# Down projection: sums of activations by way of HBM, and 25 groups by seven products in place of 22

## The chip, the cores and the metric

The kernel runs on one core of one Trainium2 chip. The metric is the device time of one execution in microseconds (us). Five engines work in parallel, each through its own instructions in order: PE (TensorE, the matrix products), DVE (VectorE), ACT (ScalarE), POOL (GpSimd) and SP (SyncE); the last two here mostly issue DMA transfers. [...]

## The reference, cut to what matters

One block of a transformer, float32, 256 tokens, width 2048. The change touches its last part, the gated feed-forward with a causal convolution over three tokens:

```
h2 = rms_norm(x, g_ffn[l])
u = causal_depthwise_conv(h2 @ w_up[l], conv_w[l], conv_b[l])   # w_up: 2048 x 11264
u_gate, u_val = jnp.split(u, 2, axis=-1)
x = x + (jax.nn.silu(u_gate) * u_val) @ w_down[l]               # w_down: 5632 x 2048
```

Ahead of it stand three attentions, their gates and an output projection; they stay as they are.

## The kernel before, in words

**Precision.** Each float32 operand is split into a high part (cast to fp32r on ACT, "hi") and a low part (the rest, a subtraction on DVE, "lo"). A product is three matmuls: activation high x weight high, activation low x weight high, activation high x weight low. In the down projection the function `three` writes them (L1309, L1310, L1311), and `parts` writes the cast (L1304) and the subtraction (L1305) for each piece of weights, up to 128 x 1024 elements.

**Up projection** (L1207 on). 176 pieces of `w_up`, 512 KB each, are loaded by SP, split, and multiplied (L1219, L1221). After each 8 pieces the generator `conv` does the convolution of two blocks of 256 channels: `u` is the input, `y` the result, `g` the gate times the value. The high and the low part of `g` go to `aT`, the activations, which stay on the chip.

**Down projection** (PLANS, from L1245 on). The 5632 rows of `w_down` are 22 pairs of 256 rows; the 2048 output columns are two halves of 1024 (`nb` 0 and 1). So there are 44 groups (a pair, a half), each with two weight tiles of 128 x 1024. A group is done in one of two ways:

- by eight (`eight`): two tiles of rows, two halves of tokens, two halves of columns, 8 products, 24 matmuls, two loads of 512 KB, in two steps of 12 matmuls.
- by seven (`seven`): 7 products of sums in place of 8, 21 matmuls, in four steps `u0` to `u3` of 3, 6, 6 and 6 matmuls. It needs four sums of weights (T1 and T3 in one tile of 128 x 1024, T4 and T2 in another) and four sums of activations (`forms`: FS1 to FS4). Its four pieces are p0 (512 columns), p1 (1024), and the two tiles of sums.

The strings in PLANS give the order of groups, "e" by eight and "s" by seven: 8 and 14 by seven, 22 by eight.

**Sums of weights.** `weight_sums` (L1170) loads the two tiles of a group during the up projection, adds them on DVE (L1181) and writes the results to HBM through POOL (`T`). A new one begins every 7 pieces of `w_up`. All 22 groups by seven get T4 and T2 so. Twelve of them (ALL_FOUR) get T1 and T3 as well; for the other ten DVE makes T1 and T3 in the down projection by two additions (L1371, L1372), into a buffer `t13`.

**Sums of activations.** `forms(p)` makes them in the down projection: five DVE operations on the split activations (L1273 to L1277), two casts on ACT, two subtractions on DVE (L1284, L1285). The results lie in `sf` and in parts of `aT` that are not needed any more.

**What sets the order.** `steps` is a list of (prep, use). The preparation of a step (load, cast, subtraction) is written two steps ahead of its use (AHEAD = 2), and `keep` fixes loads, casts and DVE operations in the order in which they are written. Beyond that an engine runs as far ahead as its buffers let it. There are four buffers for high parts and four for low parts (SBUFS = 4, tags "hi" and "lo"): the cast of one piece waits until PE has used the piece that stands four places before it. Raw weights have four buffers (WBUFS = 4), and from the eleventh load on some more (tag "more"). The matmuls are not held to the written order; a scheduler places them when the program is built.

Of the kernel before, what the change touches and what calls it, by code (L numbers as in the profile page):

```python
# [37 lines left out]
PLANS = ("eeeee" + "se" * 5 + "sse" + "s" + "eee", "e" + "sse" * 4 + "ssse" + "sssee")  # L38
ALL_FOUR = {(0, 6), (0, 7)} | {(1, p) for p in range(14) if p not in (4, 6, 8, 11)}
# [10 lines left out]
NSEVEN = tuple(plan.count("s") for plan in PLANS)  # L50


@with_exitstack
def hybrid_block(
# [1075 lines left out]
    def conv(ps, f, s):  # L1130
# [23 lines left out]
        else:  # L1154
# [9 lines left out]
            ended.append(f)  # L1164

    ended = []
    made = {}
    asked = [(0, p) for p in range(NSEVEN[0])] + [(1, p) for p in range(NSEVEN[1])]

    def weight_sums(nb, p):  # L1170
# [11 lines left out]
        four = (nb, p) in ALL_FOUR  # L1182
        add(r[0][:, 0], r[0][:, 1])
        if four:
            add(r[0][:, 1], r[1][:, 1])
# [3 lines left out]
        made[nb, p] = [dram.tile([P, PIECE], F32, name=f"T{j}_{nb}_{p}") for j in range(1 + four)]  # L1189
        if four:  # L1190
            nc.gpsimd.dma_start(made[nb, p][1], r[0].rearrange("p b n -> p (b n)"))
# [15 lines left out]
    for f0 in range(0, FT, 4):  # L1207
        for s in range(2):
            pairs = [two_banks(f"u{f0 + i}_{s}") for i in (0, 2)]
            c0 = s * D_FF + f0 * P  # L1210
            for k in range(0, KT, 2):
# [11 lines left out]
                if asked and n_ticks[0] > 8 and n_ticks[0] % 7 == 2:  # L1223
                    adding.append([weight_sums(*asked.pop(0)), 0])
# [22 lines left out]
    FS3, FS1, FS2, FS4 = range(4)  # L1247
# [8 lines left out]
    def form_of(p, f):  # L1256
        if f == FS4:
            return pieces_of(p)[:, 0, :, 1]
        if p < 10:
            return sf[:, p, f]  # L1260
        return pieces_at(31 - p).rearrange("p k (f l q) -> p (k f) l q", f=2, l=2)[:, f]

    def forms(p):

        flat = aT[:, 2 * p : 2 * p + 3].rearrange("p k s -> p (k s)").bitcast(F32)
        v = flat[:, :1024].rearrange("p (k l t q) -> p k l t q", k=2, l=2, t=NT)
        d = sm.tile([P, 512], F32, tag="junk", bufs=2, name=f"fd_{p}").rearrange("p (f l q) -> p f l q", f=2, l=2)
        r = down_pool().tile([P, 512], F32, tag="fr", bufs=1, name=f"fr_{p}").rearrange("p (f q) -> p f q", f=4)
        g = rbc.rearrange("p (k q) -> p k q", k=2)
        two = flat[:, : 2 * 640].rearrange("p (a b) -> p a b", b=640)[:, :, :512]  # L1270
        two = two.rearrange("p a (l t q) -> p a l t q", l=2, t=NT)[:, :, :, 0]
        tt = nc.vector.tensor_tensor
        keep(tt(d, two, v[:, 0, :, 1].unsqueeze(1).to_broadcast([P, 2, 2, P]), ALU.subtract))  # L1273
        keep(tt(g, v[:, :, 0, 0], v[:, :, 1, 0], ALU.add))
        keep(tt(r[:, :2], d[:, :, 0], d[:, :, 1], ALU.add))
        keep(nc.vector.scalar_tensor_tensor(r[:, FS2], r[:, FS1], -1.0, g[:, 0], ALU.mult, ALU.subtract))
        keep(tt(r[:, FS4], r[:, FS2], g[:, 1], ALU.add))  # L1277
        yield
        to = sf[:, p] if p < 10 else form_of(p, slice(0, 3))
        last = form_of(p, FS4)  # L1280
        keep(nc.scalar.copy(to[:, :, 0], r[:, :3]))
        keep(nc.scalar.copy(last[:, 0], r[:, FS4]))
        yield
        keep(tt(to[:, :, 1], r[:, :3], to[:, :, 0].bitcast(F32), ALU.subtract))  # L1284
        keep(tt(last[:, 1], r[:, FS4], last[:, 0].bitcast(F32), ALU.subtract))  # L1285
# [3 lines left out]
    def buffer(name):  # L1289
        turn[0] += 1  # L1290
        if turn[0] > 10 and turn[0] % 3 == 0:
            return down_pool().tile([P, PIECE], F32, tag="more", bufs=2, name=name)
        return wp.tile([P, PIECE], F32, tag="raw", name=name)

    def load(src, name):
        raw = buffer(f"raw_{name}")
        keep(nc.sync.dma_start(raw[:, : src.shape[1]], src))
        return raw

# [50 lines left out]
    def seven(p, n0, X, Y, first, last):  # L1350
# [3 lines left out]
        four = (n0 // PIECE, p) in ALL_FOUR  # L1354
# [98 lines left out]
    for nb, plan in enumerate(PLANS):  # L1453
# [5 lines left out]
        if nb == 0:  # L1459
            at(-1, lambda: start(0))  # L1460
# [64 lines left out]
```

## Time and profile before

| | |
|---|---|
| three timed runs | 1471.39, 1473.31, 1473.43 us; median 1473.31 |
| profiled execution, first to last instruction (span) | 1469.9 us |
| up projection, first to last of its matmuls | 747.6 to 1241.0 us |
| down projection | 1241.0 to 1466 us |
| busy share of the span: PE, DVE, ACT, POOL | 100%, 82%, 61%, 5% |
| HBM read, written | 349.70 MB, 37.75 MB |

The page of the profile gives no other time of the profiled execution than its span; the median of the timed runs is 3.4 us longer, for what lies ahead of the first instruction and behind the last.

How to read the rows further down: a row of a timeline has the start in us, the duration in us (from the first to the end of the last where equal rows that follow each other are merged, "x2"), engine, line, operation, out<-in and the number. In brackets stands the idle time just before it and what ended that. An instruction of an engine may start before the end of the one ahead of it has been recorded, so the time that one costs its engine is the distance from start to start. A row of windows has the stretch, its length, the busy time of each engine with the number of instructions, the granted clock of PE, the busy share of the DMA engines and GB/s. A row of waits has: who waited, for whom, us in total, times, the longest.

### The profile page before, as it was taken

To read this page: it belongs to the slowest core of one execution; us is meant where nothing else is said; L and a number is where in the kernel's file an instruction comes from. 1 tells how busy PE (TensorE), PEld (TensorE's weight loads), DVE (VectorE), ACT (ScalarE), POOL (GpSimd) and SP (SyncE) were. 2 spreads that over 40 slices of the span, in tenths; PEclk is the share of its full clock that TensorE was granted. 3 is DMA by queue.
4 is the path that set the end of the run, shared out by engine and by line. 5 is a ranking of instruction groups with operands and counts; after the bars stand their busy time and mean duration, and the time that the engine had idled before them with its cause. 6 is when DMAs were issued, how large, how long until landed. Compare 5 with 4: busy or idle time off the path is not lost.

```text
span 1469.9 us, 20741 instructions
## 1 busy us (share of the span) xinstructions
PE 1462.8 (100%) x7327; PEld 1233.4 (84%) x7327; DVE 1205.1 (82%) x1617; ACT 895.3 (61%) x1287; POOL 68.8 (5%) x139
## 2 busy tenths in 40 slices
PE   9999999999999999999999999999999999999998
PEld 7888888888878888888888888888888888888887
DVE  5798767766997799888877888788887886998998
ACT  6755454454664466545657667567676777665774
POOL 1000001021000000000000000000000010000000
PEclk9999999999999999999999999999999999999999
DMA  8697898787766576866776888889888895778995
GB/s 295 202 341 260 265 313 270 226 294 267 256 221 204 204 271 247 287 222 237 273 239 218 302 272 276 294 277 310 295 265 273 280 305 190 249 256 286 334 315 191
DMA packets 163463, 388.81 MB, mean 265 GB/s; under 512 B 14016, under 2 KB 22512, under 8 KB 163360
## 3 DMA queue, kind: packets, MB, share of 16 engines
q1 hardware_dynamic: 150960, 345.34, 70.6%
q0 software_dynamic: 11648, 41.10, 7.3%
q8 instruction: 57, 0.93, 0.3%
q10 hardware_dynamic: 752, 1.06, 0.2%
q14 instruction: 46, 0.38, 0.1%
HBM read 349.70 MB, written 37.75 MB: 264 GB/s over the span
## 4 chain that ended last, share of the span: by engine, by line
PE 94%; DVE 3%; DMA 2%; issue 1%; ACT 0%; SPq 0%; DVEq 0%; ACTq 0%
PE u L1219 21%; PE u L1221 10%; PE d L1310 5%; PE d L1309 5%; PE d L1311 5%; PE g_x L769 4%; PE g_x L770 4%; PE g_x L771 4%; PE s L186 2%; PE s L188 2%; PE f L187 2%; PE f L188 2%; PE f L186 2%; PE s L187 2%; PE b L186 2%; PE b L188 2%
## 5 line engine op out<-in xcount | busy, mean ns | idle before, releaser
L1219 PE MATMUL u<-hT,hi_u 128*128 128x512 f32 x1408 | 442.6, 396 | 0.0
L1221 PEld LDWEIGHTS u<-hT,lo_u 128*128 128x128 f32 x1408 | 264.4, 188 | 63.5 <-DVE lo_u L176 1.1
L1221 PE MATMUL u<-hT,lo_u 128*128 128x256 f32 x1408 | 277.0, 278 | 0.7 <-DVE lo_u L176 0.7
L176 DVE TENSOR_TENSOR lo_u<-raw_u,hi_u 128x1024 fp32r<-128x1024 f32 x176 | 213.2, 1220 | 59.8 <-ACT hi_u L175 59.0
L175 ACT CAST hi_u<-raw_u 128x1024 fp32r<-128x1024 f32 x176 | 183.0, 1049 | 107.0 <-PE u L1219 54.6
L1219 PEld LDWEIGHTS u<-hT,hi_u 128*128 128x128 f32 x1408 | 214.5, 189 | 0.1
L764 ACT CAST hi_g<-raw_g 128x1024 fp32r<-128x1024 f32 (+1 forms) x96 | 91.1, 964 | 53.5 <-PE g_x L770 33.4
L765 DVE TENSOR_TENSOR lo_g<-raw_g,hi_g 128x1024 fp32r<-128x1024 f32 (+1 forms) x96 | 105.0, 1116 | 20.9 <-ACT hi_g L764 20.8
L769 PE MATMUL g_x<-hi_g,xT 128*128 128x512 f32 x251 | 98.8, 394 | 0.0
L770 PE MATMUL g_x<-hi_g,xT 128*128 128x512 f32 x251 | 97.7, 389 | 0.0
L771 PE MATMUL g_x<-lo_g,xT 128*128 128x512 f32 x251 | 96.3, 390 | 0.0
L1148 DVE TENSOR_TENSOR y<-y,z 128x512 f32<-128x512 f32 x88 | 60.7, 691 | 24.4 <-ACT z L1147 20.5
L1147 ACT ACTIVATE z<-u,taps 128x256 f32<-128x256 f32 x176 | 74.7, 496 | 0.0
L1309 PE MATMUL d<-hi_d,aT 128*128 128x512 f32 x176 | 68.5, 389 | 0.0
L1310 PE MATMUL d<-hi_d,aT 128*128 128x512 f32 x176 | 68.5, 389 | 0.0
L1311 PE MATMUL d<-lo_d,aT 128*128 128x512 f32 x176 | 68.1, 389 | 0.0
L175 ACT CAST hi_f<-raw_f 128x1024 fp32r<-128x1024 f32 (+1 forms) x40 | 38.6, 968 | 46.6 <-PE f L187 41.9
L186 PE MATMUL s<-hi_s,xT 128*128 128x512 f32 (+1 forms) x160 | 61.9, 387 | 0.0
L175 ACT CAST hi_b<-raw_b 128x1024 fp32r<-128x1024 f32 x32 | 33.6, 1052 | 45.2 <-PE b L187 23.5
L175 ACT CAST hi_s<-raw_s 128x1024 fp32r<-128x1024 f32 (+1 forms) x40 | 38.3, 959 | 36.8 <-PE s L187 29.3
L186 PE MATMUL f<-hi_f,xT 128*128 128x512 f32 (+1 forms) x160 | 60.4, 377 | 0.0
L188 PE MATMUL s<-lo_s,xT 128*128 128x512 f32 (+1 forms) x160 | 59.1, 369 | 0.0
(498 smaller groups left out, 3265.0 us busy)
## 6 DMA issues: line engine op xcount, KB each, us to landing
raw_u<-in_w_up_dram SPq DMA_DIRECT2D x176, 512.0 KB, 5.4
raw_g<-in_w_in_dram SPq DMA_DIRECT2D x86, 512.0 KB, 5.4
T<-r POOLq DMA_DIRECT2D x64, 512.0 KB, 6.1
r<-in_w_down_dram SPq DMA_DIRECT2D x88, 256.0 KB, 5.2
raw_d<-in_w_down_dram SPq DMA_DIRECT2D x44, 512.0 KB, 5.4
raw_f<-in_w_in_dram SPq DMA_DIRECT2D x32, 512.0 KB, 5.5
raw_s<-in_w_in_dram SPq DMA_DIRECT2D x32, 512.0 KB, 5.4
raw_s<-in_w_down_dram SPq DMA_DIRECT2D x32, 512.0 KB, 5.3
```

Source lines behind the costliest of these rows:

```text
L175: pin(nc.scalar.copy(hi[:, :m], raw[:, :m]))
L176: pin(nc.vector.tensor_tensor(lo[:, :m], raw[:, :m], hi[:, :m].bitcast(F32), ALU.subtract))
L186: nc.tensor.matmul(o, lhsT=xh, rhs=wh, start=first, stop=False)
L188: nc.tensor.matmul(o, lhsT=xh, rhs=wl, start=False, stop=last)
L769: nc.tensor.matmul(o, lhsT=a[0], rhs=w[0], start=first, stop=False)
L770: nc.tensor.matmul(o, lhsT=a[1], rhs=w[0], start=False, stop=False)
L771: nc.tensor.matmul(o, lhsT=a[0], rhs=w[1], start=False, stop=last)
L1219: nc.tensor.matmul(ps, lhsT=hi[:, j, c], rhs=hT[:, k + j, :], start=first, stop=False)
L1221: nc.tensor.matmul(ps[:, :S], lhsT=lo[:, j, c], rhs=hT[:, k + j, :S], start=False, stop=last)
L1309: nc.tensor.matmul(o, lhsT=ah, rhs=w[0], start=first, stop=False)
L1310: nc.tensor.matmul(o, lhsT=al, rhs=w[0], start=False, stop=False)
L1311: nc.tensor.matmul(o, lhsT=ah, rhs=w[1], start=False, stop=last)
```

## The change

1. Groups by seven: 10 and 15 in place of 8 and 14, so 25 in place of 22, and 19 by eight in place of 22.
2. Sums of activations: for the first 15 pairs, `conv` makes them during the up projection from the unsplit `g` (`unsplit_forms`: one DVE operation of 256 elements a partition, two of 128), into the buffer of `y`, and POOL writes them to HBM (`rform`, 256 KB a pair). In the down projection `forms(i)` loads two pairs at a time (512 KB, one load of 256 KB for the last) in SP's queue among the weights, and splits them: two casts on ACT, two subtractions on DVE. The five operations of a pair in the down projection are gone.
3. Sums of weights: seventeen groups get all four during the up projection, one group every 9 pieces of `w_up`. Eight groups (OWN) get none: DVE makes all four in the down projection by four additions in place, right behind the subtraction of p1.
4. T1 and T3 are now used before T2 and T4 (`u2` and `u3` exchanged).
5. Raw buffers: every second load from the eleventh on takes one of four more (before: every third, of two, and two of `t13`). The loads of sums of activations take them too.

```diff
-PLANS = ("eeeee" + "se" * 5 + "sse" + "s" + "eee", "e" + "sse" * 4 + "ssse" + "sssee")
+PLANS = ("eeee" + "sse" * 5 + "eee", "e" + "ssse" * 4 + "sss" + "ee")
+OWN = {(0, 1), (0, 3), (0, 5), (0, 7), (0, 9), (1, 3), (1, 7), (1, 11)}
...
             nc.vector.tensor_tensor(a[:, :, S:], g, a[:, :, :S].bitcast(F32), ALU.subtract)
             ended.append(f)
+            if f // 2 < NFORM:
+                yield 1
+                unsplit_forms(f // 2, g, y)
...
+    def unsplit_forms(p, g, y):
+        v = g.rearrange("p k (t q) -> p (k t) q", t=NT)
+        r = y.rearrange("p k (t q) -> p (k t) q", t=NT)
+        tt = nc.vector.tensor_tensor
+        tt(r[:, :2], v[:, 0:4:3], v[:, 1:2].to_broadcast([P, 2, P]), ALU.subtract)
+        nc.vector.scalar_tensor_tensor(r[:, FS2], r[:, FS1], -1.0, v[:, 0], ALU.mult, ALU.subtract)
+        tt(r[:, FS4], r[:, FS2], v[:, 2], ALU.add)
+        if p % 2 == 0:
+            rforms[p // 2] = dram.tile([P, 2, 512], F32, name=f"rform{p}")
+        nc.gpsimd.dma_start(rforms[p // 2][:, p % 2], y.rearrange("p k s -> p (k s)"))
...
-                if asked and n_ticks[0] > 8 and n_ticks[0] % 7 == 2:
+                if asked and n_ticks[0] > 8 and n_ticks[0] % 9 == 2:
...
-        if turn[0] > 10 and turn[0] % 3 == 0:
-            return down_pool().tile([P, PIECE], F32, tag="more", bufs=2, name=name)
+        if turn[0] > 10 and turn[0] % 2 == 0:
+            return down_pool().tile([P, PIECE], F32, tag="more", bufs=4, name=name)
...
+    def forms(i):
+
+        p = 2 * i
+        n = min(2, NFORM - p)
+        raw = load(rforms[i][:, :n].rearrange("p a n -> p (a n)"), f"fr_{i}")
...
+        yield 2
+        keep(nc.scalar.copy(to[:, :, :, 0], r[:, :, :3]))
+        keep(nc.scalar.copy(last[:, :, 0], r[:, :, FS4]))
+        yield
+        keep(nc.vector.tensor_tensor(to[:, :, :, 1], r[:, :, :3], to[:, :, :, 0].bitcast(F32), ALU.subtract))
+        keep(nc.vector.tensor_tensor(last[:, :, 1], r[:, :, FS4], last[:, :, 0].bitcast(F32), ALU.subtract))
...
         def p1():
             raw[1] = load(dv[:, k1, n0 : n0 + PIECE], f"s{n0}_{k1}")
             w["10"], w["11"] = parts(raw[1], f"s{n0}_{k1}")
+            if own:
+                add(raw[0][:, :512], raw[0][:, 512:])
+                add(raw[0][:, 512:], raw[1][:, 512:])
+                add(raw[1][:, 512:], raw[0][:, :512])
+                add(raw[1][:, :512], raw[1][:, 512:])
 
         def p2():
...
+            if not own:
+                raw[0] = load(made[n0 // PIECE, p][1], f"t13_{name}")
+                raw[1] = load(made[n0 // PIECE, p][0], f"t{name}")
+            w["T1"], w["T3"] = parts(raw[0], f"t13_{name}")
 
         def p3():
-            w["T1"], w["T3"] = parts(raw[3], f"t13_{name}")
+            w["T4"], w["T2"] = parts(raw[1], f"t42_{name}")
...
+            for i in range(5):
+                at((0, 3, 6, 13, 23)[i], lambda i=i: later(forms(i)))
...
+                if nb and s % 2 and s // 2 + 5 < (NFORM + 1) // 2:
+                    at(len(steps), lambda i=s // 2 + 5: later(forms(i)))
```

What this moves, on three engines.

DVE, group (0, 3) of the first half, by seven, before. Ahead of these rows stands the low part of p0. `fd`, `rbc`, `fr` are the five operations for the sums of activations of a later pair, `lo_s_7` the low part of p1, `t` the tile of T1 and T3, `lo_t` the low parts of the two tiles of sums of weights (T4 and T2 first), `sf` and `aT` the subtractions for the sums of activations.

```order
L1273 TENSOR_TENSOR fd_12332<-aT 128x512
L1274 TENSOR_TENSOR rbc<-aT 128x256
L1275 TENSOR_TENSOR fr_12333<-fd_12332 128x256
L1276 SCALAR_TENSOR_TENSOR fr_12333<-fr_12333,rbc 128x128
L1277 TENSOR_TENSOR fr_12333<-fr_12333,rbc 128x128
L1305 TENSOR_TENSOR lo_s_7_12342<-raw_s_7_12339,hi_s_7_12341 128x1024
L1371 TENSOR_TENSOR t_0_3_12361<-raw_s_6_12314 128x512
L1372 TENSOR_TENSOR t_0_3_12361<-raw_s_6_12314,raw_s_7_12339 128x512
L1305 TENSOR_TENSOR lo_t_0_3_12365<-raw_t_3_12359,hi_t_0_3_12364 128x1024
L1284 TENSOR_TENSOR sf<-fr_12333,sf 128x3x128
L1285 TENSOR_TENSOR aT<-fr_12333,aT 128x128
L1305 TENSOR_TENSOR lo_t_0_3_12374<-t_0_3_12361,hi_t_0_3_12373 128x1024
```

The same group now, with its own sums. The rows on L1359 are the four additions, in place in the raw tiles of p0 (`raw_s_6`) and p1 (`raw_s_7`).

```order
L1309 TENSOR_TENSOR lo_s_6_12226<-raw_s_6_12223,hi_s_6_12225 128x512
L1309 TENSOR_TENSOR lo_s_7_12238<-raw_s_7_12235,hi_s_7_12237 128x1024
L1359 TENSOR_TENSOR raw_s_6_12223<-raw_s_6_12223 128x512
L1359 TENSOR_TENSOR raw_s_6_12223<-raw_s_6_12223,raw_s_7_12235 128x512
L1359 TENSOR_TENSOR raw_s_7_12235<-raw_s_7_12235,raw_s_6_12223 128x512
L1359 TENSOR_TENSOR raw_s_7_12235<-raw_s_7_12235 128x512
L1309 TENSOR_TENSOR lo_t_0_3_12252<-raw_s_6_12223,hi_t_0_3_12251 128x1024
L1309 TENSOR_TENSOR lo_t_0_3_12259<-raw_s_7_12235,hi_t_0_3_12258 128x1024
L1309 TENSOR_TENSOR lo_d_30_12273<-raw_d_30_12270,hi_d_30_12272 128x1024
L1309 TENSOR_TENSOR lo_d_31_12285<-raw_d_31_12282,hi_d_31_12284 128x1024
```

Seven operations of the sums of activations are gone from here; between the low part of p1 and the first low part of sums of weights stand four additions of 512 elements in place of two, and that first low part is now T1 and T3 itself, which the additions write.

PE, the same group, from its second step's last matmul on, before (`hi_t_0_3_12364` is the tile of T4 and T2, `hi_t_0_3_12373` that of T1 and T3):

```order
L1311 MATMUL d_0_11815<-lo_s_7_12342,aT 128x512
L1309 MATMUL d_2_11817<-hi_t_0_3_12364,sf 128x512
L1310 MATMUL d_2_11817<-hi_t_0_3_12364,sf 128x512
L1311 MATMUL d_2_11817<-lo_t_0_3_12365,sf 128x512
L1309 MATMUL d_1_11816<-hi_t_0_3_12364,aT 128x512
L1310 MATMUL d_1_11816<-hi_t_0_3_12364,aT 128x512
L1311 MATMUL d_1_11816<-lo_t_0_3_12365,aT 128x512
L1309 MATMUL d_3_11818<-hi_t_0_3_12373,sf 128x512
L1310 MATMUL d_3_11818<-hi_t_0_3_12373,sf 128x512
L1311 MATMUL d_3_11818<-lo_t_0_3_12374,sf 128x512
```

and now (`hi_t_0_3_12251` is T1 and T3, `hi_t_0_3_12258` T4 and T2):

```order
L1315 MATMUL d_0_11843<-lo_s_7_12238,aT 128x512
L1313 MATMUL d_3_11846<-hi_t_0_3_12251,sf 128x512
L1314 MATMUL d_3_11846<-hi_t_0_3_12251,sf 128x512
L1313 MATMUL d_2_11845<-hi_t_0_3_12258,sf 128x512
L1315 MATMUL d_3_11846<-lo_t_0_3_12252,sf 128x512
L1313 MATMUL d_3_11846<-hi_t_0_3_12251,sf 128x512
L1314 MATMUL d_3_11846<-hi_t_0_3_12251,sf 128x512
L1315 MATMUL d_3_11846<-lo_t_0_3_12252,sf 128x512
L1314 MATMUL d_2_11845<-hi_t_0_3_12258,sf 128x512
L1315 MATMUL d_2_11845<-lo_t_0_3_12259,sf 128x512
```

T1 and T3 come first, and the scheduler has put the first matmul on the tile of T4 and T2 ahead of the first one that needs a low part of T1 and T3.

SP, the loads at the start of the down projection, before:

```order
L1297 DMA raw_d_19_11857<-in_w_down_dram 128x1024
L1297 DMA raw_d_20_11889<-in_w_down_dram 128x1024
L1297 DMA raw_d_21_11915<-in_w_down_dram 128x1024
L1297 DMA raw_d_22_11935<-in_w_down_dram 128x1024
L1297 DMA raw_d_23_11955<-in_w_down_dram 128x1024
L1297 DMA raw_d_24_11975<-in_w_down_dram 128x1024
L1297 DMA raw_d_25_12005<-in_w_down_dram 128x1024
L1297 DMA raw_s_0_12033<-in_w_down_dram 128x1024
L1297 DMA raw_s_1_12060<-in_w_down_dram 128x1024
L1297 DMA raw_t_0_12080<-T_0_0_7283 128x1024
```

and now (`raw_fr` are sums of activations, read from `rform`):

```order
L1285 DMA raw_fr_11885<-rform_7417 128x1024
L1285 DMA raw_d_23_11887<-in_w_down_dram 128x1024
L1285 DMA raw_d_24_11919<-in_w_down_dram 128x1024
L1285 DMA raw_d_25_11945<-in_w_down_dram 128x1024
L1285 DMA raw_fr_11967<-rform_7877 128x1024
L1285 DMA raw_d_26_11969<-in_w_down_dram 128x1024
L1285 DMA raw_d_27_11991<-in_w_down_dram 128x1024
L1285 DMA raw_s_0_12011<-in_w_down_dram 128x512
L1285 DMA raw_fr_12036<-rform_8331 128x1024
L1285 DMA raw_s_1_12038<-in_w_down_dram 128x1024
```

Three loads of sums of activations stand among the first twelve; the raw buffers that they take from the four come back after their subtractions on DVE. In the program's addresses the load `raw_s_1` has the buffer that the first `raw_fr` had.

More of the change, by code (lines that the diff above doesn't have):

```diff
@@ L1258, in form_of @@
             return pieces_of(p)[:, 0, :, 1]
[L1259 to L1285, printed above, removed]
+        return sf[:, p % 10, f]
     turn = [0]
@@ L1471, in hybrid_block @@
                     at(len(steps) - 1, lambda nb=nb: residual(nb))
-                if formed < ns and n_done >= 4 - 3 * nb:
-                    at(len(steps) - 2, lambda p=formed: later(forms(p)))
-                    formed += 1
-        assert s == ns and not straight and formed >= ns
+        assert s == ns and not straight
         at(len(steps) - 1, finish)
```

41 lines of the change are left out of this document (18 added, 23 removed).

## The prediction

> **What bounds the kernel now.** I read the page first, then the stretches of the two projections, the waits of PE and the chain of waits, and last one group of the down projection row by row.
>
> ```profile
> span 1469.9 us, 20741 instructions
> PE 1462.8 (100%) x7327; PEld 1233.4 (84%) x7327; DVE 1205.1 (82%) x1617; ACT 895.3 (61%) x1287; POOL 68.8 (5%) x139
> ...
> 747.60:1241.00 493.40, 492.72 (x2835) 429.74 (x2834) 395.04 (x482) 343.31 (x535) 21.45 (x40) 1.00 0.83 276
> 1241.00:1466.00 225.00, 224.64 (x992) 185.74 (x991) 208.91 (x286) 141.01 (x175) 4.33 (x8) 1.00 0.78 269
> ...
> PE u L1221 <- DVE lo_u L176: 0.7, 1, 0.7
> ...
> 1371.80 0.68 PE d L1311 x3
> ```
>
> PE is busy in 224.64 of the 225.00 us of the down projection, at a granted clock of 1.00, and in all but 0.7 us of the up projection (the one wait there, for `lo_u`). The chain of waits runs along PE's own matmuls: three take 0.68 us, one 0.227. By the plan 22 groups of 24 and 22 of 21 are 990 matmuls, and 990 x 0.227 = 224.4 us: the stretch. So a matmul taken away is worth 0.227 us, and whatever makes PE wait there costs its full wait. DVE is next, 208.91 of 225.00 us.
>
> How far DVE is ahead, in group (0, 3), by seven with two additions of its own. First DVE, then one cast on ACT that waited for a buffer, then PE.
>
> ```profile
> 1293.19 0.68 DVE L1305 TENSOR_TENSOR lo_s<-raw_s,hi_s 128x512 fp32r<-128x512 f32 x1
> 1293.79 0.68 DVE L1273 TENSOR_TENSOR fd<-aT 128x512 f32<-128x512 f32 x1
> 1294.39 0.42 DVE L1274 TENSOR_TENSOR rbc<-aT 128x256 f32<-128x256 f32 x1
> 1294.73 0.42 DVE L1275 TENSOR_TENSOR fr<-fd 128x256 f32<-128x256 f32 x1
> 1295.18 0.29 DVE L1276 SCALAR_TENSOR_TENSOR fr<-fr,rbc 128x128 f32<-128x128 f32 x1
> 1295.51 0.29 DVE L1277 TENSOR_TENSOR fr<-fr,rbc 128x128 f32<-128x128 f32 x1
> 1295.72 1.22 DVE L1305 TENSOR_TENSOR lo_s<-raw_s,hi_s 128x1024 fp32r<-128x1024 f32 x1
> 1296.85 0.68 DVE L1371 TENSOR_TENSOR t<-raw_s 128x512 f32<-128x512 f32 x1
> 1297.45 0.68 DVE L1372 TENSOR_TENSOR t<-raw_s,raw_s 128x512 f32<-128x512 f32 x1
> 1298.06 1.22 DVE L1305 TENSOR_TENSOR lo_t<-raw_t,hi_t 128x1024 fp32r<-128x1024 f32 x1
> 1299.19 0.55 DVE L1284 TENSOR_TENSOR sf<-fr,sf 128x384 fp32r<-128x384 f32 x1
> 1299.66 0.28 DVE L1285 TENSOR_TENSOR aT<-fr,aT 128x128 fp32r<-128x128 f32 x1
> 1299.97 1.23 DVE L1305 TENSOR_TENSOR lo_t<-t,hi_t 128x1024 fp32r<-128x1024 f32 x1
> ...
> 1298.89 1.05 ACT L1304 CAST hi_t<-t 128x1024 fp32r<-128x1024 f32 x1 [1.67 <-PE d L1310]
> ...
> 1298.42 0.39 PE L1310 MATMUL d<-hi_d,aT 128*128 128x512 f32 x1
> 1298.88 0.39 PE L1309 MATMUL d<-hi_s,aT 128*128 128x512 f32 x1
> 1301.37 0.39 PE L1311 MATMUL d<-lo_t,sf 128*128 128x512 f32 x1
> 1302.73 0.39 PE L1311 MATMUL d<-lo_t,sf 128*128 128x512 f32 x1
> ```
>
> From start to start DVE needs 0.60 us for 512 elements, 0.34 for 256, 1.13 for 1024. The first low part of sums ends at 1299.28 and is used at 1301.37, 2.1 us ahead; the second ends at 1301.20 and is used at 1302.73, 1.5 us ahead. The cast at 1298.89 had idled 1.67 us for PE: it waited for the last high product (1298.42) on the piece four places before, whose buffer it takes. So DVE cannot lead by more than four pieces, however idle it is.
>
> **The matmuls.** 25 in place of 22 groups by seven take away 3 x 3 = 9 matmuls: 9 x 0.227 = -2.04 us. No other part of the change takes work from PE.
>
> **The eight groups with own sums.** Here a lead of four pieces is counted out. Let T0 be the moment at which PE ends the second step of the group by seven ahead. Then the buffer for p1 comes free, its cast takes 1.05, its low part starts at T0 + 1.09, and DVE is free for the next at T0 + 2.23. Then come four additions, each on the result of the one before. What such a pair costs, the sums of weights in the up projection show:
>
> ```profile
> 979.08 0.68 DVE L1181 TENSOR_TENSOR r<-r 128x512 f32<-128x512 f32 x1
> 979.80 0.69 DVE L1181 TENSOR_TENSOR r<-r,r 128x512 f32<-128x512 f32 x1
> ```
>
> 0.72 from start to start, where the independent additions at 1296.85 and 1297.45 stand 0.60 apart. So three times 0.72 and once 0.60, 2.76: the low part of T1 and T3 starts at T0 + 4.99 and ends, 1.22 later, at T0 + 6.21. The cast of T4 and T2, whose first matmul the program puts ahead of the first on that low part, can start only after the last addition, at T0 + 5.08, and ends at 6.13. PE needs both at about T0 + 5.21: two steps of 1.36 of the group ahead, 0.68 and 1.36 of this one, and two matmuls, 0.45. So PE waits 1.0 us, in every group with own sums that follows another by seven. These are seven of eight; before (1, 3) stands one by eight, whose two steps of 2.72 put the need at T0 + 7.93, 1.7 us after the low part. 7 x 1.0 = +7.0 us. What is queued behind on DVE is as late, but the next piece is needed 2.7 us on, and a group by eight gives the lead back. The bounds: 0 if something I don't see lets p1 start 1.0 us earlier, 7 x 1.5 = 10.5 if one more subtraction (0.60) stands in the way.
>
> [...]
>
> **The sums of activations** lose on DVE their five operations per pair (0.60 + 0.34 + 0.45 + 0.33 + 0.21, 1.9 us, for 14 pairs, off PE's path) and keep the subtractions, two pairs at a time: 768 elements, about 0.87 between the 0.60 and 1.13 above, and 256, 0.34, together 1.2. They stand where they delay others. In group (0, 1) they stand between the low parts of its sums, behind its four additions: +1.2 us there. In the second half three loads' subtractions fall into runs of sevens; I take nothing for them, between 0 and 0.9 each, because the groups at which they stand have mostly loaded sums, with the leads of 1.5 and 2.1 us above.
>
> At the start the loads decide. The load of `raw_s_1` takes the buffer of the first sums of activations, so it is issued when these are split.
>
> ```profile
> 1247.85 1.23 DVE L1305 TENSOR_TENSOR lo_d<-raw_d,hi_d 128x1024 fp32r<-128x1024 f32 x1 [0.26 <-ACT hi_d L1304]
> ...
> raw_d<-in_w_down_dram SPq DMA_DIRECT2D x10, 512.0 KB, 4.7
> ```
>
> At about 1249.1 a raw buffer comes free and the load of sums is issued; 4.7 to land, 2.3 for cast and low part of what stands ahead, 1.2 for its subtractions, 4.7 for `raw_s_1`, 2.3 to split it: 1264.2. PE needs it after eight steps of 2.72, one of 0.68 and 0.45, at 1263.9. +0.3 us. If the DMA takes 0.7 more each time it is 1.7; a landing of 4.5 costs nothing. SP's queue issues in order, so behind `raw_s_1` the next loads are late too, by as much.
>
> **Queues and traffic.** In the up projection SP issues 68 loads of weights for sums in place of 88, POOL 34 writes as before and 15 of 256 KB for sums of activations: -5.2 + 3.9 = -1.3 MB. The writes land after 6.1 us:
>
> ```profile
> T<-r POOLq DMA_DIRECT2D x34, 512.0 KB, 6.1
> ```
>
> The buffer `y` comes free with that, some 6 us after the convolution; it is next needed one convolution (8 pieces, 22 us) later. DVE there loses 10 additions of 0.6 (78 become 68) and gets 15 x 0.9 (0.34, 0.33 and 0.21 above), +8 us on 395 of 493: covered, unless it meets the low part for which PE waited 0.7. I take 0, between -0.7 and +2. In the down projection SP carries 34 loads of sums of weights as before and 8 of sums of activations more, from 60.8 to 63.4 MB by the plan, 4%, a DMA share of 0.78 that becomes 0.81. That is no bound on the mean, but locally:
>
> ```profile
> 1356.00:1376.00 20.00, 20.00 (x90) 16.57 (x89) 18.98 (x31) 12.25 (x17) 3.24 (x6) 1.00 0.97 350
> ```
>
> 350 GB/s at 0.97 and PE did not wait (90 matmuls). The new second half starts with three sevens with loaded sums and one load of activations: 7.1 MB in 19.7 us, 360 GB/s. I take 0, up to +2.
>
> **The sum:** -2.04 + 7.0 + 1.2 + 0.3 = +6.5 us on the span of 1469.9, 1476.4; the median of the runs, 1473.3, lies 3.4 above the span, so 1479.8, say 1480.0.
>
> **The rivals.**
> Rival 1, not slower: no waits. DVE has less to do in the down projection (14 x 1.9 and 10 pairs of additions x 1.2 fewer, 8 x 2.8 more, and 3 x 1.7 for the extra groups by seven, whose four tiles take 4.0 in place of 2.3: some 11 us of 209), its mean lead grows, and the additions are hidden: 1473.3 - 2.0 = 1471.3, and 1470.6 if the wait for `lo_u` goes too. For it: the 11 us, and leads of 1.5 to 2.1 us today behind seven more operations. Against it: the cast at 1298.89, which shows that the lead is set by buffers and not by DVE's load. It decides where each wait is under 0.3 us (7 x 0.3 = 2.0, what the matmuls give).
> Rival 2, loads: sums of activations among the weights put several later loads late, at the start and at the start of the second half: 1.7 + 2 + the waits of later loads behind it in SP's queue, 1 to 3, on top of the forecast's 1480 in place of its 0.3: 1484 to 1487. For it: 0.97 in the window above, and the chain at 1264 with nothing to spare. Against it: four raw buffers more, and 0.78 on the mean.
> Rival 3: the chain of the additions is shorter than counted. At 0.60 each the waits are 0.64: 7 x 0.64 + 1.2 + 0.3 - 2.0 = +4.0, 1477.3; with p1's cast 0.5 early as well, half of the forecast's waits or less, 1476. For it: the independent additions at 0.60. Against it: the dependent ones at 0.72. [...]
>
> **How the numbers follow.** Forecast 0.55, rival 1 0.17, rival 2 0.15, rival 3 0.13. The forecast's own range is 1477 to 1484 (waits of 0.8 to 1.5 a group); the range of 8 in 10 reaches down to rival 1 and takes the lower part of rival 2: 1471.0 to 1486.0. 0.2% (2.9 us) is about what a measurement of this kernel can tell from no change; within it, 1470.4 to 1476.2, lie nearly all of rival 1 and some 0.06 of rivals 3 and the forecast: 0.22. Faster than 1470.4 needs all matmuls, the wait for `lo_u` and something more: 0.03. The rest, 0.75, is slower.
>
> **What the new profile would show.** If right: the count of matmuls down by 9; a wait of PE of about 1 us on the first low part of T1 and T3, or on the cast of T4 and T2, in (0, 1), (0, 3), (0, 5), (0, 7), (0, 9), (1, 7) and (1, 11), none in (1, 3); the low part of p1 starting about 1.1 us after PE's end of the second step of the group ahead; the four additions 2.76 apart. (0, 1) waits longer than the others. The up projection ends at 1241.0 as before, less at most 0.7. What would make me wrong: a cast of p1 that starts earlier than its buffer rule says, waits of PE with a DMA as their releaser, or a convolution whose operations now make PE wait in the up projection.

## The result: 1486.18 us, 0.92% slower

The changed kernel took 1486.18 us (median of 4, 1484.84 to 1488.57) against 1472.49 for the kernel before (4 runs): ratio 1.0092, 95% interval 1.0078 to 1.0106. The profiled execution has a span of 1484.5 us, 14.6 more than before; it entered the up projection at 748.6 in place of 747.6, and the executions on record differ by more than that there (747.6 to 750.6).

The windows of the two projections after the change (stretch, length, then PE, PE's weight loads, DVE, ACT, POOL, clock, DMA share, GB/s) and the waits of PE in the down projection:

```profile
748.60:1242.10 493.50, 492.70 (x2835) 429.71 (x2835) 400.90 (x517) 343.92 (x535) 27.54 (x51) 1.00 0.82 271
1242.10:1482.00 239.90, 229.69 (x984) 183.34 (x982) 199.31 (x223) 142.04 (x169) 6.46 (x12) 0.99 0.77 269
...
PE d L1313 <- ACT hi_t L1308: 6.1, 9, 1.6
PE d L1315 <- DVE lo_s L1309: 1.5, 2, 0.9
PE d L1313 <- ACT hi_s L1308: 0.7, 1, 0.7
PE d L1315 <- DVE lo_t L1309: 0.3, 1, 0.3
```

The up projection takes what it took before (493.5). The down projection, from its first matmul at 1242.2 to the end of its last at 1480.3, takes 238.1 us where 981 matmuls of 0.227 are 222.4: 15.7 us are lost, where before nothing was. DVE is *less* busy than before (199 in place of 209 us), yet the waits are for it and for the casts that follow it. The waits sum to 8.6 us only. By place, taking each step from matmul to matmul over 0.227 us as lost: 3.4 us in group (0, 0), 4.7 in (0, 1), 1.15 each in (0, 3), (0, 5), (0, 7) and (0, 9), 2.5 in the second half, and about 0.5 in crumbs.

The same group (0, 3) as ahead of the prediction: DVE, ACT, PE.

```profile
1290.21 1.23 DVE L1309 TENSOR_TENSOR lo_s<-raw_s,hi_s 128x1024 fp32r<-128x1024 f32 x1 [0.21 <-ACT hi_s L1308]
1291.35 0.68 DVE L1359 TENSOR_TENSOR raw_s<-raw_s 128x512 f32<-128x512 f32 x1
1292.07 1.42 DVE L1359 TENSOR_TENSOR raw_s<-raw_s,raw_s 128x512 f32<-128x512 f32 x2
1293.52 0.69 DVE L1359 TENSOR_TENSOR raw_s<-raw_s 128x512 f32<-128x512 f32 x1
1294.13 2.50 DVE L1309 TENSOR_TENSOR lo_t<-raw_s,hi_t 128x1024 fp32r<-128x1024 f32 x2
...
1289.13 1.05 ACT L1308 CAST hi_s<-raw_s 128x1024 fp32r<-128x1024 f32 x1 [0.47 <-PE d L1314]
1292.87 1.06 ACT L1308 CAST hi_t<-raw_s 128x1024 fp32r<-128x1024 f32 x1 [2.70 <-DVE raw_s L1359]
1294.33 1.05 ACT L1308 CAST hi_t<-raw_s 128x1024 fp32r<-128x1024 f32 x1 [0.40 <-DVE raw_s L1359]
...
1294.32 0.40 PE L1314 MATMUL d<-hi_t,sf 128*128 128x512 f32 x1
1295.42 0.50 PE L1313 MATMUL d<-hi_t,sf 128*128 128x512 f32 x1 [0.71 <-ACT hi_t L1308]
1295.76 0.39 PE L1315 MATMUL d<-lo_t,sf 128*128 128x512 f32 x1
```

The matmul after the second step of the group ahead starts at 1289.16; the cast of p1, which needs the buffer that this step frees, starts at 1289.13, released by PE. The low part starts 1.08 later, the additions stand 0.72 apart, and the cast of T4 and T2 starts right behind the last addition, 5.20 after p1's. PE waits 0.71 for it, and the step from 1294.32 to 1295.42 is 0.87 too long. The first matmul after a wait is slow too, 0.34 to the next: 0.11 more.

Group (0, 1), where most is lost, DVE and then PE:

```profile
1271.90 0.95 DVE L1300 TENSOR_TENSOR sf<-raw_fr,sf 128x768 fp32r<-128x768 f32 x1
...
1273.11 1.22 DVE L1309 TENSOR_TENSOR lo_s<-raw_s,hi_s 128x1024 fp32r<-128x1024 f32 x1
1274.24 0.69 DVE L1359 TENSOR_TENSOR raw_s<-raw_s 128x512 f32<-128x512 f32 x1
...
1274.38 0.50 PE L1315 MATMUL d<-lo_s,aT 128*128 128x512 f32 x1 [0.94 <-DVE lo_s L1309]
...
1277.14 0.80 PE L1313 MATMUL d<-hi_t,sf 128*128 128x512 f32 x1 [1.57 <-ACT hi_t L1308]
```

The subtractions of sums of activations stand ahead of the low part of p1, so that this low part and the four additions behind it are late. PE waits first for the one (0.94) and then for the cast of the sums (1.57). From 1277.14 to 1280.54 its steps are 0.35 to 0.60 us in place of 0.227: the granted clock is 0.51 there (more on this below).

The start, from SP's queue and from ACT (the casts that waited for loads):

```profile
1233.46 0.33 SPq L1285 DMA_DIRECT2D raw_fr<-rform  x1
...
1246.06 0.33 SPq L1285 DMA_DIRECT2D raw_fr<-rform  x1
1250.24 3.27 SPq L1285 DMA_DIRECT2D raw_d<-in_w_down_dram  x2
1256.36 0.33 SPq L1285 DMA_DIRECT2D raw_s<-in_w_down_dram  x1
1256.80 0.51 SPq L1285 DMA_DIRECT2D raw_fr<-rform  x1
1257.56 0.33 SPq L1285 DMA_DIRECT2D raw_s<-in_w_down_dram  x1
1257.94 1.68 SPq L1285 DMA_DIRECT2D raw_t<-T  x2
...
1264.44 1.05 ACT L1308 CAST hi_s<-raw_s 128x1024 fp32r<-128x1024 f32 x1 [1.73 <-DMA raw_s<-in_w_down_dram]
1267.04 1.05 ACT L1308 CAST hi_t<-raw_t 128x1024 fp32r<-128x1024 f32 x1 [1.54 <-DMA raw_t<-T]
...
1264.00:1268.00 4.00, 2.74 (x10) 1.32 (x8) 2.43 (x3) 2.01 (x2) 0.00 (x0) 1.00 1.03 411
```

After the two loads at 1250.24 SP issued nothing until 1256.4, and then eight loads in under seven us, two of them sums of activations. The DMA engines were full (1.03, 411 GB/s, and 1.00 to 1.03 from 1260 on), and the load of `raw_s_1`, issued at 1257.56, was split only from 1264.44 on: 6.9 us, not 4.7.

### The profile page after: what moved, and what is told of

It is laid out like the page before. It is cut to its first block, busy times and chain, and to the rows that moved or that the text cites. A ratio compares the mean times of both kernels' runs of the same rounds, so it can differ in the third digit from the quotient of the medians.

```text
span 1484.5 us, 20738 instructions
## 1 busy us (share of the span) xinstructions
PE 1467.6 (99%) x7318; PEld 1230.9 (83%) x7318; DVE 1201.1 (81%) x1588; ACT 897.2 (60%) x1281; POOL 77.0 (5%) x154
## 4 chain that ended last, share of the span: by engine, by line
PE 88%; DVE 5%; DMA 4%; ACT 2%; issue 1%; SPq 0%; DVEq 0%; ACTq 0%
PE u L1234 22%; PE u L1236 11%; PE g_x L770 4%; PE g_x L771 4%; PE g_x L772 4%; PE d L1313 3%; PE d L1315 3%; PE d L1314 3%; PE f L187 2%; PE f L188 2%; PE f L189 2%; PE b L187 2%; PE b L188 2%; PE b L189 2%; PE o_x L772 2%; PE o_x L770 1%
## 5 line engine op out<-in xcount | busy, mean ns | idle before, releaser
L1313 PE MATMUL d<-hi_d,aT 128*128 128x512 f32 x152 | 59.2, 389 | 0.0
L1314 PE MATMUL d<-hi_d,aT 128*128 128x512 f32 x152 | 59.2, 389 | 0.0
L189 PE MATMUL f<-lo_f,xT 128*128 128x512 f32 (+1 forms) x160 | 59.0, 369 | 0.0
```

The costliest lines, as they stand in the source:

```text
L189: nc.tensor.matmul(o, lhsT=xh, rhs=wl, start=False, stop=last)
L1313: nc.tensor.matmul(o, lhsT=ah, rhs=w[0], start=first, stop=False)
L1314: nc.tensor.matmul(o, lhsT=al, rhs=w[0], start=False, stop=False)
```

## The experiments

All times are compared with runs of the kernel before on the same chip (medians 1471.9 to 1472.3).

**No additions.**

```diff
-            if own:
-                add(raw[0][:, :512], raw[0][:, 512:])
-                add(raw[0][:, 512:], raw[1][:, 512:])
-                add(raw[1][:, 512:], raw[0][:, :512])
-                add(raw[1][:, :512], raw[1][:, 512:])
```

> The changed kernel without the four additions of the eight groups with own sums: those groups cast and subtract the weights themselves in the place of their sums, so the sums of weights are left out there. All else is as in the changed kernel, the loads and the order too. Theory 1: the waits of these groups go wholly (low part of T1 and T3 2.8 us sooner), 6.3 us and the 1.7 + 1.8 of (0, 1): 1475 to 1478; 3.4 us stay at (0, 0), where no additions are. Rival (the waits come from the loads and casts of these groups, not from the additions): over 1483.

1472.70 us, ratio 1.0009 (1.0001 to 1.0018), where the changed kernel had 1.0092: the additions of eight groups are 0.83 of the 0.92%, some 12 us. This kernel leaves out the sums of weights of eight groups. In its trace no wait at the sums of these groups is left; 3.0 us stay lost in (0, 0), about as expected (3.4), and 0.7 in (0, 1). The time is below what was expected: half of what I had left to (0, 1) and nearly all that was lost in the second half went with the additions, some 1.7 us with the 0.4 of (0, 0). The other 2 us the trace does not show, for its execution took 1474.87, 2.2 above the median.

**Own sums behind a group by eight.**

```diff
-OWN = {(0, 1), (0, 3), (0, 5), (0, 7), (0, 9), (1, 3), (1, 7), (1, 11)}
+OWN = {(0, 2), (0, 4), (0, 6), (0, 8), (1, 3), (1, 6), (1, 9), (1, 12)}
```

> The changed kernel with one line edited: the eight groups with own sums are other ones, each right behind a group by eight: (0, 2), (0, 4), (0, 6), (0, 8), (1, 3), (1, 6), (1, 9), (1, 12). Same work on every engine, same loads in number. Theory 1 (the lead of four pieces, used up where a group by seven stands ahead): the waits at the cast of T4 and T2 go, 1.15 us each at (0, 3), (0, 5), (0, 7), (0, 9), 0.96 at (1, 7), 0.69 at (1, 11), together 6.3, and of what is lost in (0, 1) the 1.7 at its own sums and the 1.8 of the slower clock behind it: 1475.5 to 1478, with 3.4 us still lost at (0, 0). Rival (the four additions cost DVE time that PE misses wherever they stand): 1486, the waits now in the new groups.

1481.73, ratio 1.0067 (1.0055 to 1.0079): half of the gain that was expected. (0, 6) and (0, 8) do not wait, but (0, 2) loses 1.8 us, (0, 4) 2.7 and the second half 3.3. The rows of (0, 4), one cast on ACT and then DVE, say why:

```profile
1295.05 0.62 ACT L1308 CAST hi_s<-raw_s 128x512 fp32r<-128x512 f32 x1 [1.84 <-DMA raw_s<-in_w_down_dram]
...
1301.02 0.69 DVE L1359 TENSOR_TENSOR raw_s<-raw_s 128x512 f32<-128x512 f32 x1
1301.63 0.95 DVE L1300 TENSOR_TENSOR sf<-raw_fr,sf 128x768 fp32r<-128x768 f32 x1
1302.50 0.42 DVE L1301 TENSOR_TENSOR aT<-raw_fr,aT 128x256 fp32r<-128x256 f32 x1
1302.83 2.35 DVE L1309 TENSOR_TENSOR lo_t<-raw_s,hi_t 128x1024 fp32r<-128x1024 f32 x2
```

Behind the last addition stand now the subtractions of the sums of activations, 1.2 us, and only then the low part that PE needs; PE waits 0.7 for it. That is the last of three waits: 0.4 and 0.7 us ahead of it are for the casts of the two tiles of sums. Their additions were late because p0 had been split late (its cast waited 1.84 us for its load) and the casts of the sums of activations stood on ACT between p0 and p1. Sums of weights and sums of activations had met in one group, as they did in (0, 1) of the changed kernel.

**Loads of sums of activations late.**

```diff
-                at((0, 3, 6, 13, 23)[i], lambda i=i: later(forms(i)))
+                at((0, 9, 19, 29, 39)[i], lambda i=i: later(forms(i)))
```

> The changed kernel with the loads of sums of activations of the first half asked for after steps 0, 9, 19, 29, 39 in place of 0, 3, 6, 13, 23, each about nine steps before its first use. The own sums stay where they are. Theory 2 (at the start the second and third of these loads stand in SP's queue between weights that are needed sooner, in a burst that keeps the DMA at a share of 1.0): of the 8.1 us lost between 1264 and 1281 the 3.4 of group (0, 0) fall under 1, the 1.1 ahead of (0, 1)'s low part of p1 goes and the slower clock with it; the own sums of (0, 1) still wait about 1.2: 1480 to 1482. Rival (the first of these loads alone is to blame, by the raw buffer that it keeps): 1484 to 1486, and the load of raw_s_1 is issued after 1257 as now.

1486.81, ratio 1.0104 (1.0086 to 1.0121): no gain, and above both ranges. The 3.4 us of (0, 0) went as theory 2 said (no wait before 1269). But (0, 3) and (0, 5) lost 3.0 and 3.9 us in place of 1.15 (1.3 of the 3.9 at a lower granted clock), and (0, 1) still 3.4; (0, 7) lost 1.7 and (0, 9) 1.1. Two things changed in (0, 3) and (0, 5): the casts of the sums of activations stand on ACT between those of T1, T3 and T4, T2, and p1 was split 1.4 us later than its buffer allowed. In (0, 5) the cast of p1 had waited for its load (0.69 us, until 1302.76); in (0, 3) the trace names PE for it, but the cast of p0 just ahead had waited 2.38 us for its load. So a late load is shown for the one and likely for the other.

**Both edits together.**

> The two edits together: own sums only behind groups by eight, and the loads of sums of activations late. Theories 1 and 2: no wait of PE over 0.5 us is left in the down projection in its first half, and 0.8 us at most in the second (0.24 and 0.55 us are lost there now at places where sums of activations are split): 1470.4 (nine matmuls less than before, nothing given back) to 1472.5, faster than before or the same. If the own sums cost wherever they stand, 1481 or more; if the first load of sums of activations is to blame, 1474 to 1476.

1474.58, ratio 1.0018 (1.0009 to 1.0026). By the medians the first edit alone was worth 4.5 us, the second -0.6, both together 11.6; with each taken against the kernel before on its own chip, 3.9, -1.2 and 11.0. The waits of PE in the down projection are down to 1.4 us, in six places, and the stretch is 226.5 us, 4.1 above the matmuls.

**Late loads, no additions** (the two edits above that are named so).

> The changed kernel without the four additions (the sums of weights of the eight groups are left out) and with the loads of sums of activations late, after steps 0, 9, 19, 29, 39. In the run with late loads alone the waits at (0, 0) were gone but those of the own sums had doubled, to 2.3 us and more a group, since the subtractions of the sums of activations (1.2 us) then stand ahead of the additions. Theory 3 (a wait arises only where 1.2 us of subtractions or 2.8 us of additions meet a group by seven behind another by seven, and the late loads themselves are harmless): no wait over 0.3 us in the first half, 1469.5 to 1471.0. Rival (the late loads cost of themselves): above 1472.7, the time without additions and with early loads.

```profile
1241.10:1466.00 224.90, 223.59 (x984) 183.75 (x982) 178.95 (x191) 142.44 (x169) 4.32 (x8) 1.00 0.79 282
PE d L1315 <- DVE lo_d L1309: 0.3, 1, 0.3
```

1470.97 against 1472.28, ratio 0.9990 (0.9981 to 0.9999). Here the nine matmuls show, 1.3 us of the 2.04 by the medians (0.1 to 2.8 by the interval), and the loads of sums of activations cost nothing that can be measured: one wait of 0.3 us. (In the run with late loads alone the subtractions stood behind both low parts of (0, 3), at 1292.62, and not ahead of the additions, as the expectation has it.)

**Fewer own sums, so more sums in the up projection.** Four groups, 21 groups' sums one every 8 pieces, and three groups, 22 groups' sums one every 7.

```diff
+OWN = {(0, 4), (0, 8), (1, 3), (1, 12)}      # four; three: {(1, 3), (1, 6), (1, 12)}
...
+                if asked and n_ticks[0] > 8 and n_ticks[0] % 8 == 2:      # three: % 7
...
+                at((0, 13, 15, 33, 34)[i], lambda i=i: later(forms(i)))      # three: (0, 13, 23, 33, 43)
```

> Complete version: own sums only in (0, 4), (0, 8), (1, 3) and (1, 12), each behind a group by eight; 21 groups' sums made in the up projection, one every 8 pieces; loads of sums of activations after steps 0, 13, 15, 33, 34 of the first half and 26, 28, 40 of the second, so that their subtractions fall in groups by eight ahead of which no own sums are prepared. Theory 3: no wait left in the down projection, 1470.0 to 1471.5, 1 to 2 us faster than before. Rival: the traffic of the up projection (8.4 MB more than with 17 groups) brings waits there, or two loads of sums close together bring some here: 1472 to 1475.

> As the version with four own groups, but with three, all in the second half: (1, 3), (1, 6), (1, 12); 22 groups' sums made in the up projection, one every 7 pieces as before the change; loads of sums of activations one at a time, after steps 0, 13, 23, 33, 43 of the first half and 12, 40, 42 of the second. Theory 3: 1470.0 to 1471.5 as well; the nine matmuls are worth 2.0 us and nothing is given back. Rival: sums of activations that fall in the same group by eight as own sums, (1, 3) and (1, 12), bring 0.3 to 0.9 us each: 1471 to 1473.

1491.09, ratio 1.0116 (1.0102 to 1.0131), and 1477.94, ratio 1.0040 (1.0025 to 1.0054). The rival named for four groups, waits in the up projection, was right in kind, but far too low in its time (1472 to 1475). With three own groups (an execution of 1483.19, the slowest of six), the window and the waits of the up projection, and what its casts waited for (the idle time ahead of the casts and subtractions that read the loads of `w_up`, by what ended it: us, times):

```profile
747.00:1250.00 503.00, 498.34 (x2846) 432.57 (x2845) 412.71 (x540) 344.24 (x534) 35.23 (x65) 1.00 0.87 291
PE u L1236 <- DVE lo_u L177: 4.5, 5, 2.4
...
  DMA raw_u<-in_w_up_dram: 66.0, 45
```

In the kernel before they waited for these loads 24 times, 37.9 us (changed kernel: 21 times, 32.0 us), and one low part came too late for PE; now 45 times, 66.0 us, and five came too late. The up projection took 500.5 us (750.3 to 1250.8) in place of 493.5, with four own groups 504.1 (749.1 to 1253.2). So five more groups' sums do not fit there for nothing, at a DMA share of 0.87 in place of 0.82. The amount alone does not set the price: with four own groups there is one group's sums less, a share of 0.84, and yet the casts waited 100.9 us for these loads and PE 15 times, 7.5 us. There the sums began every 8 pieces, in step with the convolution, and the last were still being added at 1250, against 1205 with three own groups; in the down projection 9.2 us were lost, nearly all in its first half. No run separates the spacing from the amount.

**The rest of the lateness: loads of the second half moved, subtractions on POOL, both.**

```diff
-        keep(nc.vector.tensor_tensor(to[:, :, :, 1], ...
+        keep(nc.gpsimd.tensor_tensor(to[:, :, :, 1], ...
```

> The version with both edits (own sums behind groups by eight, late loads) and, in the second half, the three loads of sums of activations after steps 22, 36 and 50 in place of 10, 20 and 28. In the version with both edits 4 us are still lost in the down projection, 1.3 of them at (1, 3) to (1, 5), where the 1.2 us of subtractions stand on DVE just ahead of the additions of (1, 3). Theory 3: those go, 1473 to 1474. Rival (what is left there is the first run of sevens, not the subtractions): 1474.6 as before.

> The version with both edits, and the two subtractions of each load of sums of activations on POOL in place of DVE (loads where they were). POOL has nothing else to do there; how long it takes no run shows (its operations of 128 elements in the kernel before took 0.3 to 0.5 us, so 768 may take 2 to 3; the first use is some seven steps later in the first half, later still in the second). Theory 3 (DVE's subtractions are what is left of the lateness): no wait over 0.3 us in the down projection, 1470.5 to 1472. Rival (what is left is the loads' landing, or POOL slows DVE while it works): 1474 or more.

> The last two together: both edits, loads of the second half moved, subtractions on POOL. Theory 3: 1470.3 to 1471.8, the best of all if POOL's subtractions are in time; a gain over the kernel before of 0.5 to 2 us, the nine matmuls at most. Rival (POOL slows DVE, or is late): as the version with the subtractions on POOL alone.

1474.64, ratio 1.0012 (1.0003 to 1.0021); 1481.48, ratio 1.0061 (1.0048 to 1.0073); 1479.09, ratio 1.0044 (1.0032 to 1.0057). Moving the loads cleared (1, 3) to (1, 5), 1.6 us in the version with both edits, but other places lost as much, most of it in the first half, which this edit does not touch (1.0 us at 1276, 0.9 at 1314). POOL made it worse: its own operations, by group, and the subtraction on DVE beside them (shortest, median, longest).

```profile
L1300 POOL TENSOR_TENSOR sf<-raw_fr,sf 128x768 fp32r<-128x768 f32 x7 | 16.4, 2342 | 128.2 <-ACT sf L1297 128.2
L1301 POOL TENSOR_TENSOR aT<-raw_fr,aT 128x256 fp32r<-128x256 f32 x7 | 11.0, 1566 | 0.0
...
L1309 DVE TENSOR_TENSOR lo_t<-raw_t,hi_t x34: 1210/1224/2153, 1266.1 to 1460.9; 128x1024 fp32r<-128x1024 f32 x34
...
1274.25 2.15 POOL L1300 TENSOR_TENSOR sf<-raw_fr,sf 128x768 fp32r<-128x768 f32 x1 [14.60 <-ACT sf L1297]
...
1275.45 2.02 DVE L1309 TENSOR_TENSOR lo_t<-raw_t,hi_t 128x1024 fp32r<-128x1024 f32 x1 [0.77 <-ACT hi_t L1308]
```

Four times in the first half a DVE subtraction of 1024 elements starts while POOL's first one is running, and takes 2.02 to 2.15 us in place of 1.22. Each of the four ends 1.07 to 1.09 us after POOL's, whatever its own start, as if it had begun only then (POOL's, begun at 1274.25, ends at 1276.40, and the one recorded from 1275.45 on ends at 1277.47), while one begun at 1273.46, already running when POOL's began, kept its 1.22. The 0.80 to 0.93 us more stand inside the recorded time of the subtraction, not ahead of it; what holds it up there no run shows.

**A fifth buffer**, paid for with two of the four extra raw buffers.

```diff
-            return down_pool().tile([P, PIECE], F32, tag="more", bufs=4, name=name)
+            return down_pool().tile([P, PIECE], F32, tag="more", bufs=2, name=name)
...
+        fifth = turn[0] > 10 and split[0] % 5 == 0
+        pool, x = (down_pool(), "5") if fifth else (wp, "")
+        hi = pool.tile([P, PIECE], F32R, tag="hi" + x, bufs=1 if fifth else SBUFS, name=f"hi_{name}")
...
```

> The changed kernel with a fifth buffer for high and low parts in the down projection (every fifth piece takes it), paid for with two of the four extra raw buffers. Own sums and loads stand as in the changed kernel. Theory 1 (four buffers bound the lead, and the additions need 1.0 us more than that): every cast comes a step, 1.36 us, sooner, and the waits at (0, 3), (0, 5), (0, 7), (0, 9), (1, 7), (1, 11) go, 6.3 us: 1478 to 1481, with the start as bad as it is or worse, since two raw buffers are gone. Rival (DVE or the loads are the bound, not the buffers): the waits stay at 0.7 to 0.9 us a group, 1485 or more.

1538.46, ratio 1.0442 (1.0425 to 1.0458). It doesn't answer the question: with two raw buffers fewer PE waited 33 us, in 39 places, mostly for casts of late loads, and the granted clock of the down projection was 0.94, though no wait was above 1.8 us. What the fifth buffer did and what the two missing ones cost can't be told apart. More lead by buffers without that price was not tried.

**One long wait in the kernel before.**

```diff
+            if (n0, p) == (0, 3):
+                z = sm.tile([P, 512], F32, tag="junk", bufs=2, name="z")
+                for i in range(12):
+                    keep(nc.vector.tensor_tensor(z, z if i else raw[0][:, :512], raw[0][:, 512:], ALU.add))
             w["T4"], w["T2"] = parts(raw[2], f"t42_{name}")
```

> The kernel before with twelve dependent additions of 512 elements (results unused) in DVE's queue ahead of the low part of T4 and T2 of one group, (0, 3): one long wait of PE in the middle of a projection that has none, to price a wait by itself. 12 x 0.72 = 8.6 us, less the lead of 2.1: PE waits about 6.5. Theory 4 (a wait costs its length, about 0.3 us of restart, and, where PE has been idle for some us shortly before, a stretch at a lower granted clock, as between 1276 and 1282 in the changed kernel, 1.8 us): the stretch of the down projection grows by 8 to 9. Rival (the lower clock there had nothing to do with idleness): by 6.5 to 7, with the clock at 1.00 throughout.

```profile
1309.89 0.79 PE L1311 MATMUL d<-lo_t,sf 128*128 128x512 f32 x1 [5.03 <-DVE lo_t L1305]
1310.48 0.63 PE L1311 MATMUL d<-lo_t,aT 128*128 128x512 f32 x1
1310.91 0.63 PE L1309 MATMUL d<-hi_d,aT 128*128 128x512 f32 x1
...
1309.80:1313.80 4.00, 3.91 (x9) 2.88 (x10) 4.00 (x6) 1.03 (x2) 0.00 (x0) 0.51 0.90 317
1313.80:1318.00 4.20, 4.20 (x20) 3.43 (x20) 4.13 (x9) 2.30 (x4) 0.00 (x0) 1.00 0.85 297
```

1480.81 us in one run (1472.28 for the kernel before). PE waited 5.0 us, less than the 6.5 expected (the program had put other matmuls ahead), and the stretch grew by 7.2: for the next 3.7 us the granted clock was about half (0.51 in that window) and a matmul took 0.43 to 0.59, 1.9 us lost after the wait. So the theory on the slower clock holds in this one run. In the changed kernel the same came without one long wait:

```profile
1274.00:1278.00 4.00, 2.05 (x6) 1.17 (x6) 3.88 (x6) 1.83 (x2) 0.00 (x0) 0.88 0.85 274
1278.00:1282.00 4.00, 4.00 (x13) 3.03 (x13) 4.00 (x5) 3.73 (x7) 0.00 (x0) 0.69 0.53 173
```

There PE had lost 5.7 us in six pieces between 1264 and 1277, none above 1.6 us of waiting. The slow stretch is about as long in both runs, 3.7 us there and 3.4 here (1277.14 to 1280.54). In the changed kernel only gaps of 1.6 us and less, close together, stand ahead of it. Short gaps don't always bring it: in the run with late loads alone PE waited 1.26 and 0.70 us in (0, 3) and 1.29 and 0.70 in (0, 5), and behind the first pair the clock stayed, behind the second it fell:

```profile
1291.00:1295.00 4.00, 3.88 (x16) 2.82 (x16) 3.53 (x5) 3.81 (x5) 0.00 (x0) 1.00 0.32 101
1309.90:1313.30 3.40, 3.40 (x10) 2.71 (x9) 3.40 (x5) 3.08 (x4) 0.00 (x0) 0.52 0.39 116
```

So the length of the waits alone does not decide, and what does was not measured.

## Why the prediction was wrong

The direction and the main place were right, the size was half: +6.5 us forecast, +13.7 measured, and 1486.18 lies 0.2 above the range. That it came so near is luck of the step from span to time: the 3.4 us for what lies ahead of the first instruction and behind the last are too much. Nearly every execution with both on record took 1.7 to 1.8 us more than its span (the changed kernel 1486.25 and 1484.5); the rest of the 3.4 was that the span came from an execution faster than the median of the first three runs. On the span the forecast was 1476.4, and 8.1 short. Two terms of the sum failed, (0, 1) and the start.

- *Matmuls, -2.04.* As forecast: 981 in the trace, and 1.3 us faster where little else is lost (late loads, no additions).
- *Own sums, +7.0.* The chain from T0 came out to within 0.15 us (5.20 for 5.08 at the cast of T4 and T2), and it was this cast that PE waited for. The lateness was 0.87 to 0.89 in the first half. What was missing is what a wait costs beside its length: slow first matmuls, so that a group lost 1.15. (1, 7) and (1, 11) lost 1.07 and 0.69. Without (0, 1) that is 6.4 us for 6.0 forecast. (1, 3) shows no wait, as forecast, though its subtractions of sums of activations stood ahead of p1's low part there too, and two steps were 0.24 too long together.
- *(0, 1), 1.0 + 1.2.* This term failed: 4.7 us. Its subtractions did not stand behind the additions but ahead of them and of p1's low part, at 1271.90, and pieces already late from (0, 0) reached it. So it lost 1.2 us at p1's low part and 1.7 at the cast of its first sums, 2.9 for the 2.2 forecast, and then 1.8 us through the slower clock, which the prediction had not at all.
- *The start, +0.3.* This term failed: 3.4 us. That `raw_s_1` is issued when the first sums of activations are split was right, and the time was too (subtractions done at 1257.5 for 1257.3), but by luck: their load was issued at 1233.46 and not at 1249.1, and then they waited for their places on ACT (1251.40) and on DVE (1256.25, behind a low part whose weights had landed late). The step that made the loss is the landing, 4.7 us taken from loads of the kernel before, whose DMA was not full there (a share of 0.60 between 1241 and 1262). The loads that were held back behind it all came at once, two of sums of activations with them: 6.9. The bound given, 0.7 more, was too narrow; rival 2 had named the mechanism.
- *The second half, 0.* Some 0.8 us beside (1, 7) and (1, 11): 0.24 at 1396, in (1, 3), and 0.55 at 1407, inside the bounds given.
- *The up projection, 0.* As forecast: 493.5 us for 493.4, one wait of 0.8 us.
- *Rivals 1 and 3.* The waits are there, and the additions at 1291.35, 1292.07 and (after the merged pair) 1293.52 stand 0.72 apart and not 0.60, so neither rival's chain holds. *Rival 2* came true at the start, beside the forecast's own waits. The time lies in its range of 1484 to 1487, but in part by luck: nothing was lost at the start of the second half, which it had named too, and without additions 3.7 us are all that the loads cost.

What the sum left out is that lateness adds up along a group: each term was priced as if it stood alone. In the experiments the two edits were worth 4.5 and -0.6 us apart and 11.6 together.

## What to carry to other kernels

Where buffers and not load set the lead of an engine, its mean busy time says nothing about waits (DVE's fell from 209 to 199 us in the down projection, and PE waited 8.6): count the chain from the release of the buffer to the use, with every operation in the queue between. Two small jobs that each fit into the slack of a group don't fit together; look where they meet before pricing them. Price a wait of a full PE above its length: in these runs by some 0.3 us for a short one (0.87 us late cost 1.15 in (0, 3)), and by 1.3 to 1.9 us more where the clock fell behind it (it did behind one wait of 5.0 us and behind some groups of short ones, not behind all). And take a load's landing from a window in which the DMA is as full as it will be then (here 4.7 us was taken from before, where its share was 0.60 at this place, and 6.9 came at 1.00 to 1.03).

Of the versions that leave nothing out none beats the kernel before: the best two, both edits with and without the moved loads of the second half, are 0.12% and 0.18% slower, and in the places that were tried the additions cost more than the nine matmuls bring.

## What the runs showed of the hardware

Three things I had not expected: the clock of PE fell to about half not only after one wait of 5.0 us (0.51, the kernel before with a long wait) but after six short ones (5.7 us lost in 13; 0.51, the changed kernel), and in the run with late loads alone after one pair of 1.3 and 0.7 us (0.52) but not after a pair just like it (1.00); the first matmul after a wait of 0.7 us took 0.34 to the next in place of 0.227; and a DVE subtraction of 1024 elements that started while POOL subtracted took up to 2.15 us in place of 1.22, and ended 1.07 to 1.09 us after POOL's (in the version with both edits and the subtractions on POOL).
